# Eight neighbouring weight rows to a partition, 8 KB stage buffers, and another final norm, in a one-core mixture-of-experts block

## The chip, the cores and the metric

The kernel runs on one core of a Trainium2 chip. Its engines are TensorE (PE, with PEld for the weight loads), VectorE (DVE), ScalarE (ACT), GpSimd (POOL) and SyncE (SP, which here only issues DMAs and reads registers). The metric is the device time of one execution in microseconds; lower is better.

## What is computed

A block on x of 2048 tokens by 1024 columns, all float32: a convolution mixer and a gated DeltaNet, an output projection with a residual, a mixture of experts, and a final norm. The change touches the loading of the expert weights, the operand that goes with them, and the final norm:

```python
x = x + jnp.concatenate([y_a, y_b], axis=-1) @ w_out[l]
h = rms_norm(x, ffn_norm_g[l]).reshape(Bsz * S, D)
x = x + hier_moe(h, router_group_w[l], router_expert_w[l], w_gate[l], w_up[l], w_down[l]).reshape(Bsz, S, D)
...
return rms_norm(x, final_norm_g)

def hier_moe(h, ...):
    # a group of 4 is chosen for each token, then the top 2 of its 8 experts: 32 experts in all
    ...
        a = xblk @ w_gate[e]        # [tokens, 1024] @ [1024, 512]
        b = xblk @ w_up[e]
        return (jax.nn.silu(a) * b) @ w_down[e]     # [tokens, 512] @ [512, 1024]
```

## The kernel before

The program has five stretches (times of the profiled execution): projections, DeltaNet and mixers to about 940 us; the output projection, 940 to 1150; routing, to 1187; the expert loop, to 1875; the end of the final norm, to 1951. P is 128 partitions, D 1024, KT = 8 blocks of 128 columns of D, FF 512, NT = 16 token tiles.

**Precision.** Each product is made from float16 pieces. `split` (lines 91 to 93) writes the high piece with ACT (L92: a scaled copy) and then the low piece with DVE (L93: source times scale minus the high piece). Three matmuls take the place of one.

**Output projection.** A loop over 16 token tiles. `tile_a(t)` multiplies by `wo` in two halves of 512 columns (L965), adds the halves to the tile of x on DVE (L970), squares on ACT, writes the sum to DRAM `acc_d`, makes the scale `ss` on POOL (L978), and splits x times `ss` into `hh` (L979), which SP writes to `h2_d`. `tile_b(t - 1)` transposes `hh` and multiplies by the router weights `wr`. SP loads the next tile of x ahead of each. From tile 10 on, `hid` runs `load_picked` beside the tiles, five steps to a tile: it loads the first two experts, picked from the tokens seen by then.

**Weights of an expert.** `load_part` (L757) has three parts: the first and the second half of gate and up (8 steps), and down (4 steps). A step takes one stage buffer of 128 partitions by 4 KB from `stage()`, has SP load it from DRAM, and calls `split` into the float16 tile `wgu` or `wd`. Gate and up are viewed as "(k p) f": partition p gets row k*128 + p, so one step has two DMAs of 128 rows of 2 KB, a gate half and an up half. Down has one DMA of 128 rows of 4 KB. `gw` holds the norm's gain times WS, one column for each k. The pool `mst` has five buffers; after the output projection `mst2` brings five more on the other side of memory, and `stage()` takes them in turn. SP works its queue in order: a DMA that waits for its buffer holds up every DMA written behind it.

**Expert loop.** 32 jobs, one for each expert, by rising number from the two early ones. `weave` interleaves generators by the shares given with each: in job j, `gate_up(J)` (L1045) beside the rest of the weights of job j + 1, then `down(J)` (L1080, L1115) beside the first part of job j + 2. POOL gathers each job's rows of `h2_d` and scatter-adds its result `yo` to `acc_d` (L1058). Each scatter-add waits for the one before.

**Final norm.** `norm_all` (L1339) loads the 16 tiles of `acc_d` with POOL's indirect DMAs (L1347) through index columns `bix`, which leave out the tokens of the last three jobs; it first loads AHEAD = 8 tiles into eight stage buffers. Then come, for each four tiles, the squares, the root and the gains, and the stores: SP for tiles 0 to 11 (L1369), POOL for 12 to 15 (L1371). Behind the store of tile t the load of tile t + 8 is written, in the next stage buffer. That load waits until the store that last read this buffer has landed, and behind `gathers[0]`, the gather of the rows of job 30. The rows of those tokens are done apart: `rows_of` (L1379) gathers them, `norm_rows` and `store_rows` (L1390) finish them; `last_rows` puts the two middle jobs' rows, of 120 and 116 tokens ("ends"), behind the first store of POOL; the last job's 112 rows ("base") come at the very end. Each of these three stores waits for the one before to land, as a token may belong to two of the jobs.

## Time and profile before

| what | us |
|---|---|
| median of three runs | 1953.33 (1951.74 to 1954.88) |
| the profiled execution's own time | 1952.58 |
| its span in the trace | 1950.8 |
| PE busy over the span | 1747.4 (90%) |
| DVE busy | 1402.0 (72%) |
| ACT busy | 1008.3 (52%) |
| POOL busy | 436.7 (22%) |

Execution and span lie 1.8 us apart; a difference read in the span is a difference of the execution. The shares of the whole span say little here, since the stretches have different limits: the table of busy time by stretch has to be read, and inside a stretch the chain of waits, which follows the work that ended last back from its end. PEclk is TensorE's granted clock, 1.00 being 2.4 GHz. The DMA share is the mean busy share of the core's sixteen DMA engines, as their packet records give it; it goes a few hundredths over 1.

### The profile page before, as it was taken

The numbers are of one execution on the slowest core, as the hardware profiler recorded it, in microseconds if no ns is written. First come the engines' busy times: TensorE is split into PE (matmuls) and PEld (weight loads), VectorE is DVE, ScalarE is ACT, GpSimd is POOL, SyncE is SP. The second block draws the span as 40 slices with busy tenths as digits, with TensorE's granted clock in tenths as the row PEclk, the third lists the DMA queues.
The fourth block names the chain that finished last, engine by engine and source line by source line (L and its number), as shares of the span: only waits on it lengthen the run. The fifth ranks groups of instructions, "written<-read, shape, count | busy, mean of one in ns | idle before, by whom it ended". The sixth has DMA issues, their size and how long they took to land.

```text
span 1950.8 us, 41817 instructions
## 1 busy us (share of the span) xinstructions
PE 1747.4 (90%) x16213; PEld 1197.7 (61%) x16213; DVE 1402.0 (72%) x2708; ACT 1008.3 (52%) x1674; POOL 436.7 (22%) x375
## 2 busy tenths in 40 slices
PE   6789999999999999999999869899889999999830
PEld 5455555555555554444454438798888899999730
DVE  8889888888888745322344768787778888888722
ACT  6655434444444324211233636676667877777631
POOL 1321111121121100000000013233222344344343
PEclk9889999999999999999999979999999999999975
DMA  4222002001001105002255967999999999999873
GB/s 143 67 69 52 11 16 52 9 13 45 20 10 37 36 18 165 22 17 60 98 174 182 343 236 254 342 302 312 305 312 346 360 343 343 344 349 309 290 228 140
DMA packets 203597, 330.27 MB, mean 169 GB/s; under 512 B 44590, under 2 KB 98935, under 8 KB 203394
## 3 DMA queue, kind: packets, MB, share of 16 engines
q1 hardware_dynamic: 178738, 271.20, 40.7%
q0 software_dynamic: 20128, 47.30, 9.7%
q10 hardware_dynamic: 4528, 9.06, 1.2%
q8 instruction: 129, 2.11, 0.4%
q14 instruction: 74, 0.61, 0.1%
HBM read 276.05 MB, written 54.82 MB: 170 GB/s over the span
## 4 chain that ended last, share of the span: by engine, by line
PE 35%; DMA 15%; DVE 7%; issue 5%; ACT 3%; SPq 1%; POOL 1%; POOLq 0%; ACTq 0%; DVEq 0%
PE a L1045 12%; PE acc L134 11%; DMA mst<-in_w_up_dram 7%; PE a L965 5%; DMA mst<-in_w_down_dram 4%; DVE wgu L93 2%; ACT wgu L92 1%; DMA mst<-in_w_gate_dram 1%; DMA mst<-acc_d,bix 1%; SPq L766 1%; PE pn L548 1%; PE pl L1102 1%; PE pl L1080 1%; DVE xT L1031 1%; DMA wst<-in_w_out_dram 1%
## 5 line engine op out<-in xcount | busy, mean ns | idle before, releaser
L134 PE MATMUL acc<-hT,whl 128*128 128x512 f16 x2640 | 636.5, 381 | 0.2 <-DVE hT L203 0.2
L134 PEld LDWEIGHTS <-whl 128*128 128x128 f16 x2640 | 253.3, 99 | 249.6 <-issue 13.4
L1045 PE MATMUL a<-xT,wgu 128*128 128x128 f16 (+17 forms) x6144 | 393.8, 227 | 5.0 <-DVE sl L1052 4.1
L1045 PEld LDWEIGHTS <-wgu 128*128 128x128 f16 x6144 | 388.3, 99 | 11.3 <-issue 5.3
L93 DVE SCALAR_TENSOR_TENSOR wgu<-mst,gw,wgu 128x1024 f16<-128x1024 f32 x256 | 317.3, 1276 | 20.7 <-ACT wgu L92 17.9
L92 ACT ACTIVATE wgu<-mst,gw 128x1024 f16<-128x1024 f32 x256 | 280.1, 1139 | 32.6 <-DMA mst<-in_w_up_dram 30.1
L965 PE MATMUL a<-wo,yb 128*128 128x512 f16 x768 | 175.8, 380 | 0.0
L1058 POOL DMA_INDIRECT acc_d<-yo,tabS x50 | 101.5, 2031 | 253.9 <-ACT yo L1106 189.8
L93 DVE SCALAR_TENSOR_TENSOR wd<-mst,wd 128x1024 f16<-128x1024 f32 x128 | 154.1, 1214 | 5.0 <-ACT wd L92 5.0
L92 ACT ACTIVATE wd<-mst 128x1024 f16<-128x1024 f32 x128 | 131.0, 1047 | 22.2 <-DMA mst<-in_w_down_dram 21.4
L1115 PE MATMUL a<-ac,wd 128*128 128x144 f16 (+12 forms) x1824 | 136.2, 230 | 1.3 <-ACT ac L92 1.2
L1115 PEld LDWEIGHTS <-wd 128*128 128x128 f16 x1824 | 124.2, 98 | 4.0 <-issue 2.3
L965 PEld LDWEIGHTS <-yb 128*128 128x128 f16 x768 | 72.0, 98 | 79.2 <-issue 2.4
L294 DVE SCALAR_TENSOR_TENSOR cv<-raw,pcol,cv 128x512 f32<-128x512 f32 x144 | 117.9, 821 | 1.6
L1014 POOL DMA_INDIRECT xr<-h_d,tabG x51 | 59.6, 1168 | 168.9 <-PE t L1030 162.8
L1052 DVE SCALAR_TENSOR_TENSOR sl<-a,sl 128x128 f32<-128x128 f32 (+17 forms) x128 | 38.3, 300 | 78.8 <-ACT sl L1051 78.3
L1051 ACT ACTIVATE sl<-a 128x128 f32<-128x128 f32 (+17 forms) x128 | 35.9, 281 | 113.7 <-PE a L1045 112.9
L382 DVE TENSOR_TENSOR pr<-Ts,fs 32x1 f32<-32x1 f32 (+14 forms) x240 | 77.7, 324 | 3.9 <-DMA fs<-dscr 0.2
L1019 POOL DMA_INDIRECT gs<-gt_d,gix x51 | 74.0, 1451 | 15.6 <-issue 15.3
L1102 PE MATMUL pl<-id,yt 128*128 128x128 f32 (+13 forms) x304 | 53.3, 296 | 25.1 <-ACT yo L1106 20.9
L545 ACT ACTIVATE osq<-acv 128x512 f32<-128x512 f32 x16 | 10.0, 627 | 126.1 <-DVE acv L543 126.1
L1080 PE MATMUL pl<-wd,ac 128*128 128x512 f16 (+4 forms) x312 | 75.0, 387 | 0.2 <-DVE ac L93 0.2
(348 smaller groups left out, 2539.3 us busy)
## 6 DMA issues: line engine op xcount, KB each, us to landing
mst<-in_w_gate_dram SPq DMA_DIRECT2D x256, 256.0 KB
mst<-in_w_up_dram SPq DMA_DIRECT2D x256, 256.0 KB
mst<-in_w_down_dram SPq DMA_DIRECT2D x128, 512.0 KB
wst<-in_w_in_dram SPq DMA_DIRECT2D x28, 512.0 KB
xt<-in_x_dram SPq DMA_DIRECT2D x16, 512.0 KB
ydr<-yh SPq DMA_DIRECT2D x64, 128.0 KB
x<-in_x_dram SPq DMA_DIRECT2D x16, 512.0 KB
yb<-ydr SPq DMA_DIRECT2D x16, 512.0 KB
```

The costliest lines, as they stand in the source:

```text
L92: A.activation(hi, src, AF.Copy, scale=scale)
L93: (eng or V).scalar_tensor_tensor(lo, src, scale, hi, op0=OP.mult, op1=OP.subtract)
L134: T.matmul(acc, w[:, i, k, :], hT[b][:, j, k, :], start=(n == 0), stop=(n == 3 * KT - 1))
L294: V.scalar_tensor_tensor(y, tap(j), pcol[:, q:q + 1], y, op0=OP.mult, op1=OP.add)
L382: V.tensor_tensor(q, Ts[:, 0:i, 0:i].rearrange("p j m -> p m j"), bc(fs[:, None, 0:i, i], [32, i, i]), op=OP.mult)
L965: T.matmul(po, yb[:, i, k, c * P:(c + 1) * P], wo[:, j, k, n * FF:(n + 1) * FF], start=(q == 0), stop=(q == 3 * KT - 1))
L1019: G.indirect_dma_start(out=g[0:cw], out_offset=None, in_=gt_d[0:end * NE, :], in_offset=IO(ap=gx, axis=0))
L1045: T.matmul(pg[:, q, 0:n], wq[:, i, k, q, f * P:(f + 1) * P], xT[:, j, k, 0:n], start=(z == 0), stop=(z == 3 * KT - 1))
L1058: st = G.indirect_dma_start(out=acc_d, out_offset=IO(ap=sx, axis=0), in_=yo[0:cw], in_offset=None, bounds_check=S - 1, oob_is_err=False, c ...
L1080: T.matmul(py[0:n], ac[:, i, k, 0:n], wd[:, j, k, q * FF:(q + 1) * FF], start=(z == 0), stop=(z == 3 * FF // P - 1))
L1102: T.transpose(py[0:cw, c * P:(c + 1) * P], yts[d2][:, u, off:off + cw], id32)
L1115: T.matmul(pg[:, u, 0:n], wd[:, i, k, d * P:(d + 1) * P], ac[:, j, k, 0:n], start=(z == 0), stop=(z == 3 * FF // P - 1))
```

## The change

Three things are done. **Weights:** gate and up are viewed as "(p k) f", so that partition p holds the eight neighbouring rows 8p to 8p + 7. A step of two k then loads 2 x 2 KB that lie side by side in DRAM, one piece of 4 KB for each partition, and a stage buffer is [128, 2, 1024], 8 KB a partition. An expert has 4 DMAs for gate, 4 for up (of 512 KB each, where 8 of 256 KB stood) and 4 for down as before, in pairs to a buffer. `mst` has two such buffers (five of 4 KB before), `mst2` three (five before), and the turn among them is mst, mst2, mst2, mst, mst2. **What goes with them:** k now numbers columns 8p + k of h, so the gains `gw` are loaded in that order by a DMA of their own, the router's weights too, and the split of `hh` reads the tile of x in steps of eight columns (32 bytes) and writes it in rows. **Final norm:** tiles 0 to 7 are loaded in pairs to a stage buffer (`load_early`); tiles 8 to 15 all go into one tile `xw`, which takes a buffer of `wgu` after the last expert's weights (`load_late`), so none waits for a store. The squares, gains and stores of tiles 0 to 3 move ahead of the scatter of job 30, tile 4's store is made to wait for that scatter, and at the end `rest()` does the ends' norms, tiles 8 to 11, the base rows' norm, tiles 12 to 15, and then the stores of the three ends.

```diff
-    mst = moe.enter_context(tc.tile_pool(name="mst", bufs=5, reuse_waits="tile"))
+    mst = moe.enter_context(tc.tile_pool(name="mst", bufs=2, reuse_waits="tile"))
...
-        return pool.tile([P, D], F32, name="mst")
+        return pool.tile([P, 2, D], F32, name="mst")
...
-            vs = [src[0][ds(e, 1)].rearrange("o (k p) f -> p (o k) f", p=P) for src in (w_gate, w_up)]
-            for k in range(i * KT // 2, (i + 1) * KT // 2):
-                st = stage().rearrange("p (q f) -> p q f", q=2)
+            vs = [src[0][ds(e, 1)].rearrange("o (p k) f -> p (o k) f", k=KT) for src in (w_gate, w_up)]
+            for k in range(i * KT // 2, (i + 1) * KT // 2, 2):
+                st = stage().rearrange("p q (k f) -> p q k f", k=2)
                 for q in range(2):
-                    lastw[0] = nc.sync.dma_start(st[:, q], vs[q][:, k, :]).ins
-                split(w[:, 0, k], w[:, 1, k], st, gw[:, k:k + 1])
-                yield 1
+                    lastw[0] = nc.sync.dma_start(st[:, q], vs[q][:, k:k + 2, :]).ins
+                for d in range(2):
+                    split(w[:, 0, k + d], w[:, 1, k + d], st[:, :, d], gw[:, k + d:k + d + 1])
+                    yield 1
...
-            for k in range(FF // P):
+            for k in range(0, FF // P, 2):
                 st = stage()
-                lastw[0] = nc.sync.dma_start(st, v[:, k, :]).ins
-                split(w[:, 0, k], w[:, 1, k], st, WS)
-                yield 1
+                for d in range(2):
+                    lastw[0] = nc.sync.dma_start(st[:, d], v[:, k + d, :]).ins
+                for d in range(2):
+                    split(w[:, 0, k + d], w[:, 1, k + d], st[:, d], WS)
+                    yield 1
...
-        split(hh[:, 0], hh[:, 1], x1, ss)
+        split(*(hh[:, i].rearrange("p (k q) -> p k q", k=KT) for i in range(2)), x1.rearrange("p (q k) -> p k q", k=KT), ss)
...
-    mst2 = moe.enter_context(tc.tile_pool(name="mst2", bufs=5, side="right", reuse_waits="tile"))
-    stages[:] = [mst, mst2]
+    mst2 = moe.enter_context(tc.tile_pool(name="mst2", bufs=3, side="right", reuse_waits="tile"))
+    stages[:] = [mst, mst2, mst2, mst, mst2]
...
+    def load_early():
         for t in range(AHEAD):
+            if t % 2 == 0:
+                pair = stage()
+            xs[t] = pair[:, t % 2]
             load(t)
             yield 1
+
+    def load_late():
+
+        w = mw.tile([P, NT - AHEAD, D], F32, name="xw", tag="wgu")
+        with tc.issue_after(gathers[0]):
+            for t in range(AHEAD, NT):
+                xs[t] = w[:, t - AHEAD]
+                load(t)
...
                 if t < NPL:
-                    nc.sync.dma_start(out2[t * P:(t + 1) * P, :], x)
+                    st = nc.sync.dma_start(out2[t * P:(t + 1) * P, :], xs[t])
+                    if t == GT:
+                        tc.add_manual_dep(st.ins, adds[-1].ins.name, SYNC, reason="the scatter goes first")
...
-                load(t + AHEAD)
...
+    def rest():
+        for x, sx in ends:
+            norm_rows(x)
+        yield from slices(na, 2 * GT)
+        norm_rows(J.base[0][0:J.n], end)
+        yield from slices(na, 2 * GT)
+        for x, sx in ends + [(end, J.chunks[0][2])]:
+            store_rows(x, sx)
```

How the instructions move is shown at three places. **POOL at the last scatter-adds**, as the kernel before has them: L1058 is the scatter-add of job 30, L1379 the gathers of the last jobs' rows, L1347 a load of a token tile, L1334 a root, L1400 the base rows' scatter:

```order
L1058 DMA acc_d<-yo,tabS 2048x1024
L1379 DMA mst<-acc_d,tabG 112x1024
L1379 DMA end<-acc_d,tabG 120x1024
L1379 DMA end<-acc_d,tabG 116x1024
L1347 DMA mst<-acc_d,bix 128x1024 x4
L1334 TENSOR_TENSOR ss_24316<-ss_24316,mhalf 128x4
L1347 DMA mst<-acc_d,bix 128x1024 x2
L1334 TENSOR_TENSOR ss_24429<-ss_24429,mhalf 128x4
L1347 DMA mst<-acc_d,bix 128x1024 x2
L1400 DMA acc_d<-mst,tabS 2048x1024
```

And in the changed kernel (L1063, L1392, L1347, L1339 and L1413 are the same instructions):

```order
L1063 DMA acc_d<-yo,tabS 2048x1024
L1339 TENSOR_TENSOR ss_23741<-ss_23741,mhalf 128x4
L1392 DMA mst<-acc_d,tabG 112x1024
L1392 DMA end<-acc_d,tabG 120x1024
L1392 DMA end<-acc_d,tabG 116x1024
L1347 DMA xw<-acc_d,bix 128x1024 x8
L1413 DMA acc_d<-mst,tabS 2048x1024
```

The eight loads of late tiles now stand in one row behind the gathers, with no root between them.

**POOL at its end**, before: L1371 is a store of a token tile, L1390 a store of an end's rows, L1334 a root:

```order
L1334 TENSOR_TENSOR ss_24472<-ss_24472,mhalf 128x4
L1334 TENSOR_TENSOR ss_24487<-ss_24487,mhalf 120x1
L1371 DMA out_dram<-mst,bix 2048x1024
L1334 TENSOR_TENSOR ss_24493<-ss_24493,mhalf 116x1
L1390 DMA out_dram<-end,tabS 2048x1024
L1371 DMA out_dram<-mst,bix 2048x1024 x2
L1390 DMA out_dram<-end,tabS 2048x1024
L1371 DMA out_dram<-mst,bix 2048x1024
L1334 TENSOR_TENSOR ss_24518<-ss_24518,mhalf 112x1
L1390 DMA out_dram<-mst,tabS 2048x1024
```

And in the changed kernel (L1385 and L1403 are those stores):

```order
L1339 TENSOR_TENSOR ss_23995<-ss_23995,mhalf 120x1
L1339 TENSOR_TENSOR ss_24001<-ss_24001,mhalf 116x1
L1339 TENSOR_TENSOR ss_24007<-ss_24007,mhalf 128x4
L1339 TENSOR_TENSOR ss_24026<-ss_24026,mhalf 112x1
L1339 TENSOR_TENSOR ss_24032<-ss_24032,mhalf 128x4
L1385 DMA out_dram<-xw,bix 2048x1024 x4
L1403 DMA out_dram<-end,tabS 2048x1024 x2
L1403 DMA out_dram<-mst,tabS 2048x1024
```

All roots now stand ahead of all stores, and the three stores of the ends stand last, behind four stores of tiles, where the first of them stood behind one.

**DVE in the output projection beside the load of the picked experts**, before: L970 adds a half of the product to x, L93 makes the low piece of `hh` or of `wgu`, L1000 makes a tile's logits:

```order
L970 SCALAR_TENSOR_TENSOR x_9719<-a,x_9719 128x512
L977 TENSOR_SCALAR ss_10020<-ss_10020 128x1
L93 SCALAR_TENSOR_TENSOR hh<-x_9719,ss_10020,hh 128x1024
L93 SCALAR_TENSOR_TENSOR wgu<-mst,gw,wgu 128x1024
L970 SCALAR_TENSOR_TENSOR x_9888<-a,x_9888 128x512
L93 SCALAR_TENSOR_TENSOR wgu<-mst,gw,wgu 128x1024
L1000 SCALAR_TENSOR_TENSOR L<-pl,lt 128x36
L970 SCALAR_TENSOR_TENSOR x_9888<-a,x_9888 128x512
L93 SCALAR_TENSOR_TENSOR wgu<-mst,gw,wgu 128x1024
L977 TENSOR_SCALAR ss_10162<-ss_10162 128x1
L93 SCALAR_TENSOR_TENSOR wgu<-mst,gw,wgu 128x1024 x2
```

And in the changed kernel (L974 and L1005 are L970 and L1000):

```order
L974 SCALAR_TENSOR_TENSOR x_9719<-a,x_9719 128x512
L981 TENSOR_SCALAR ss_10020<-ss_10020 128x1
L93 SCALAR_TENSOR_TENSOR hh<-x_9719,ss_10020,hh 128x1024
L974 SCALAR_TENSOR_TENSOR x_9888<-a,x_9888 128x512
L93 SCALAR_TENSOR_TENSOR wgu<-mst,gw,wgu 128x1024 x2
L1005 SCALAR_TENSOR_TENSOR L<-pl,lt 128x36
L974 SCALAR_TENSOR_TENSOR x_9888<-a,x_9888 128x512
L981 TENSOR_SCALAR ss_10156<-ss_10156 128x1
L93 SCALAR_TENSOR_TENSOR wgu<-mst,gw,wgu 128x1024 x2
L974 SCALAR_TENSOR_TENSOR x_10028<-a,x_10028 128x512
L93 SCALAR_TENSOR_TENSOR wgu<-mst,gw,wgu 128x1024
```

The pieces of `wgu` now come two in a row from one buffer, where they came singly.

## Rows read from the trace of the kernel before

**Rows 1.** The page's first line.
```profile
span 1950.8 us, 41817 instructions
```

**Rows 2.** Busy time by stretch, all engines; columns in the first line.
```profile
core 0: us, PE busy (x) PEld busy (x) DVE busy (x) ACT busy (x) POOL busy (x), PEclk, DMA share, GB/s
...
1050.00:1170.00 120.00, 93.62 (x652) 48.24 (x651) 81.11 (x216) 61.88 (x78) 11.21 (x15) 0.88 0.77 273
...
1187.00:1500.00 313.00, 289.81 (x3705) 260.96 (x3704) 252.22 (x333) 221.13 (x312) 91.25 (x57) 0.96 0.99 320
...
1500.00:1800.00 300.00, 294.89 (x4535) 281.01 (x4533) 261.23 (x380) 227.98 (x330) 122.41 (x79) 1.00 1.02 344
...
1875.00:1951.00 76.00, 0.00 (x0) 0.00 (x0) 20.40 (x22) 12.31 (x22) 30.81 (x25) 0.51 0.52 170
```

**Rows 3.** Chain that ended last, 1040 to 1200: start, us, what.
```profile
1054.30 1.28 DVE hh L93
...
1069.81 7.44 DMA x<-in_x_dram
...
1090.88 9.18 DMA mst<-in_w_down_dram
...
1120.22 5.48 DMA mst<-in_w_down_dram
...
1147.27 1.30 DVE hh L93
```

**Rows 4.** Busy time in three 2-us stretches, columns as rows 2.
```profile
1077.00:1079.00 2.00, 2.00 (x11) 0.90 (x10) 0.69 (x1) 1.10 (x2) 0.00 (x0) 1.00 1.04 400
...
1326.50:1328.50 2.00, 2.00 (x38) 2.00 (x37) 0.84 (x1) 2.00 (x4) 1.55 (x1) 0.97 1.06 408
...
1086.50:1088.50 2.00, 2.00 (x12) 0.91 (x10) 2.00 (x3) 2.00 (x4) 0.00 (x0) 1.00 1.03 420
```

**Rows 5.** Timeline of SP's queue, 1835 to the end: start, us, instruction.
```profile
1861.76 47.74 SPq L1369 DMA_DIRECT2D out_dram<-mst  x12
```

**Rows 6.** DVE by line and shape, 100 to 700: count | busy, mean ns.
```profile
L382 DVE TENSOR_TENSOR pr<-Ts,fs 32x64 f32<-32x64 f32 x16 | 4.0, 253 | 0.3
...
L382 DVE TENSOR_TENSOR pr<-Ts,fs 32x225 f32<-32x225 f32 x16 | 9.5, 597 | 0.1
```

**Rows 7.** All engines by line and shape, 940 to 1160.
```profile
L93 DVE SCALAR_TENSOR_TENSOR hh<-x,ss,hh 128x1024 f16<-128x1024 f32 x16 | 20.5, 1283 | 20.3 <-ACT hh L92 20.3
...
L92 ACT ACTIVATE hh<-x,ss 128x1024 f16<-128x1024 f32 x16 | 18.3, 1146 | 13.1 <-POOL ss L978 13.1
```

**Rows 8.** By line, 1187 to 1850; behind the bar's second: idle before, releaser.
```profile
L93 DVE SCALAR_TENSOR_TENSOR wgu<-mst,gw,wgu 128x1024 f16<-128x1024 f32 x239 | 295.8, 1276 | 14.5 <-ACT wgu L92 11.9 <-DMA mst<-in_w_gate_dram 2.4
...
L92 ACT ACTIVATE wgu<-mst,gw 128x1024 f16<-128x1024 f32 x238 | 260.2, 1139 | 27.5 <-DMA mst<-in_w_up_dram 25.2 <-DMA mst<-in_w_gate_dram 0.8
```

**Rows 9.** Timeline of POOL from 1838 to the end; brackets: idle before, releaser.
```profile
1879.60 0.98 POOL L1379 DMA_INDIRECT mst<-acc_d,tabG  x1 [15.83 <-DMA acc_d<-yo,tabS]
...
1883.77 1.04 POOL L1347 DMA_INDIRECT mst<-acc_d,bix  x1 [0.30 <-issue]
...
1899.15 1.02 POOL L1347 DMA_INDIRECT mst<-acc_d,bix  x1 [7.10 <-DMA out_dram<-mst]
...
1906.79 2.03 POOL L1347 DMA_INDIRECT mst<-acc_d,bix  x1 [0.30 <-issue]
...
1924.22 2.02 POOL L1390 DMA_INDIRECT out_dram<-end,tabS  x1 [0.23 <-issue]
...
1930.27 1.27 POOL L1390 DMA_INDIRECT out_dram<-end,tabS  x1 [1.41 <-issue]
...
1940.26 1.01 POOL L1390 DMA_INDIRECT out_dram<-mst,tabS  x1 [6.84 <-issue]
```

More of the change, by code (lines that the diff above doesn't have):

```diff
@@ L1246, in overflow @@
         for dst, row in ((cp_, capE), (rk, nov)):
-            pq = stage(mst).rearrange("p (k t e) -> p k t e", k=2, e=NE)
+            pq = stage(mst)[:, 0].rearrange("p (k t e) -> p k t e", k=2, e=NE)
             V.tensor_tensor(pq, OH, bc(row[:, None, None, :], sh), op=OP.mult)
@@ L1276, in overflow @@
         for q in range(2):
-            big = stage(mst).rearrange("p (a b) -> p a b", a=NE)
+            big = stage(mst)[:, 0].rearrange("p (a b) -> p a b", a=NE)
             V.tensor_tensor(big, bc(iot[:, q * NE:(q + 1) * NE, None], sh), bc(oend[:, None, :], sh), op=OP.is_ge)
@@ L1337, in gain, with load, norm_all @@
         V.scalar_tensor_tensor(x if dst is None else dst, x, s, gfin[0:n], op0=OP.mult, op1=OP.mult)
-    def norm_all():
-        xs = {}
-        def load(t):
-            if t < NT:
-                xs[t] = stage()
-                hold = tc.issue_after(gathers[0]) if t >= AHEAD else nullcontext()
-                with hold:
-                    st = G.indirect_dma_start(out=xs[t], out_offset=None, in_=acc_d,
-                                              in_offset=IO(ap=bix[:, t:t + 1], axis=0), bounds_check=S - 1,
-                                              oob_is_err=False)
-                apart(st, adds)
-                for o in sums:
-                    tc.add_manual_dep(st.ins, o.ins.name, SYNC, reason="the sums of the experts before")
-                loads.append(st)
+    xs = {}
+    def load(t):
+        st = G.indirect_dma_start(out=xs[t], out_offset=None, in_=acc_d, in_offset=IO(ap=bix[:, t:t + 1], axis=0),
+                                  bounds_check=S - 1, oob_is_err=False)
+        apart(st, adds)
+        for o in sums:
+            tc.add_manual_dep(st.ins, o.ins.name, SYNC, reason="the sums of the experts before")
+        loads.append(st)
+    def load_early():
         for t in range(AHEAD):
+            if t % 2 == 0:
+                pair = stage()
+            xs[t] = pair[:, t % 2]
             load(t)
             yield 1
+    def load_late():
[4 more added lines that the diff above has]
+                load(t)
+    def norm_all():
         for t0 in range(0, NT, GT):
@@ L1425, in behind @@
             yield z
-    def last_rows(na, ends):
-        for _ in na:
-            if len(stores) == 1 and not outs:
-                for x, sx in ends:
-                    norm_rows(x)
-                for x, sx in ends:
-                    store_rows(x, sx)
-            yield 1
     eids = {}
@@ L1508, in hybrid_block @@
         if left == LAST:
[L1509 to L1511 removed]
+            parts.append((slices(firsts, 4), 4, WE, 1))
         weave(*parts)
[L1513 removed]
+        if left in (LAST, 1):
             marks.append(latest())
[L1515 to L1518 removed]
+    end = stage()[0:J.n, 0]
+    def rest():
[6 more added lines that the diff above has]
+            store_rows(x, sx)
+    drain(behind(rest(), marks[-1]))
     nb_ = nc.values_load(nblk[0:1, 0:1], min_val=0, max_val=NB2)
@@ L1529, in hybrid_block @@
         add(J)
-        x = rows_of(ox[:, 1:2], P, stage())
+        x = rows_of(ox[:, 1:2], P, stage()[:, 0])
         norm_rows(x)
```

51 lines of the change are left out of this document (20 added, 31 removed).

## The prediction

> **What bounds the kernel now.** The page's first line gives the span [rows 1]; the table of busy time by stretch is read next, since the stretches have different limits [rows 2]. In the expert loop two limits stand close together. From 1187 to 1500 the DMA share is 0.99 and PE is busy 289.81 of 313 us at a granted clock of 0.96; from 1500 to 1800 PE is busy 294.89 of 300 while the DMA share is 1.02. So what shortens transfers can pay in the first of these and hardly in the second. In the end of the output projection (1050 to 1170) neither is full: PE 93.62 of 120, DMA 0.77. There the chain of waits has to be read [rows 3]: it runs over the landing of a tile of x (7.44 us), of down pieces (9.18 and 5.48), and over the split of `hh` on DVE. From 1875 on PE has nothing to do, and the end is a chain of POOL's transfers, read from POOL's timeline [rows 9].
>
> **The end of the final norm.** POOL stands 15.83 us until the scatter of job 30 has landed, then issues the gathers and the late loads [rows 9]. The first late load starts at 1883.77 and each takes 1.04 and 0.30 of issue. But the sixth waits 7.10 us for a store, at 1899.15, and the last starts at 1906.79, since the later loads need buffers that stores must free. With `xw` the eight run in a row: the last starts at 1883.77 + 7 x 1.34 = 1893.2, 13.6 us sooner. Against that, four tile stores instead of one now stand ahead of the first end's store: 3 x (1.02 + 0.30) = 4.0 later. What is behind stays: 6.05 from the first end's store to the second (1924.22 to 1930.27), 9.99 to the third (1940.26), 10.5 to the end of the span. Third, the stores of tiles 0 to 3, which began at 1861.76 [rows 5] and moved while POOL stood for the scatter, now come before it, and tiles 4 and on wait for it: 2.1 MB, 5.1 us at the 408 GB/s of [rows 4], are out of its way; I take 2 of the 5. Sum -13.6 + 4.0 - 2 = -11.6, taken as **-12**. Ends: if the second interval shrinks to the first's 6.05, as no tile store stands between, and the scatter gains 4, it is -9.6 - 3.9 - 4 = -17.5, so -18; if the ends' stores find their queue full it is -1 (a rival, below).
>
> **Pieces of 4 KB.** In two saturated stretches of 2 us, rows of 2 KB went at 408 GB/s, and in one where rows of 4 KB filled the queue it was 420, the share at its top in both (1.06 and 1.03) [rows 4]. An expert's gate and up are 4.19 MB: 10.28 us at 408, 9.99 at 420, so 0.29 an expert. 239 splits of `wgu` at 8 an expert are 30 experts [rows 8], 8.8 us if every one were bound by the transfer. The second stretch is bound by PE, so about half is to be had: **-5** (-9 to 0; 0 since the stretch's mean of 320 [rows 2] lies well under 408, so that something other than the packet rate may set it). The four DMA issues an expert that SP saves are worth nothing, as SP waits for buffers anyway.
>
> **Coarser stage buffers.** A buffer of 4 KB is held for a split, 1.139 on ACT and then 1.276 on DVE [rows 8], 2.4 us. One of 8 KB is held for two, which overlap: 1.139 + 2 x 1.276 = 3.7. So 1.3 us more pass until a buffer takes its next load. Five buffers of 1 MB stand for ten of 512 KB, 5.2 MB either way, 12.8 us of queue at 408; the 1.3 us should mostly be covered by the other four. What is late if not is ACT, which already stood 25.2 us for up pieces in this stretch [rows 8]. I take **+3**, an eighth of that; 0 if all is covered, +8 if the wait grows by a third.
>
> **The split of `hh` in steps of 32 bytes.** DVE's product in L382 reads both its sources in steps of 64 bytes: 253 ns for 64 elements, 597 for 225 [rows 6], so 344 / 161 = 2.14 ns an element. The split of `hh` takes 1283 ns for 1024 elements in a row [rows 7]; at 2.14 it is 2.19 us, 0.9 more. All sixteen grow, but up to 1050 PE hides them. Five stand on the chain from 1040 to 1150, the first at 1054.30, the last at 1147.27 [rows 3]: **+4**. The trace has no such read on ACT; its piece is 1146 ns [rows 7]. If it grows by 0.9 too the sum is +9; if four of five find cover in the landings between, +1. The Trainium skill, "Vector Engine (DVE) Microarchitecture Reference", section 5.2, tells of this cost: single words that hop on one source take 1.73 ns a column, where pairs or rows take 1.05. [Rows 6] have two such sources, at 2.14. By the page's figure the split would be 0.6 longer, my estimate, and this term +3.
>
> **Two experts through two buffers.** Until 1170 only `mst` is there: two of 8 KB, where five of 4 KB were. The queue is deep there: a piece of 512 KB needs 1.28 us at 408, but 9.18 passed from its issue to its landing [rows 3]. With 2.1 MB outstanding instead of 2.6 the queue is 1.3 us shorter, and the tile of x behind it lands sooner; but SP stands longer for a buffer with that x written behind it, and both pieces of a buffer land before either is split. The three landings shown are 22.1 us. I take **+3**; if they grow by half it is +11, taken as +12 with the second wait for `hh`, and if they shrink by a quarter, -6. The DMA for `gw` and the new view of the router's weights are small and lie before 940, behind projections: 0. The extra wait of tile 4's store for the scatter holds up only SP's stores behind it, which the late loads no longer need: 0, with the tail's range for what they cost on the queue.
>
> Sum: -12 - 5 + 3 + 4 + 3 = -7. From the profiled execution, 1952.58, that gives 1945.6; the median of the three runs lies 0.75 above it, so **1946** as a median.
>
> **Rivals.**
> *The preload stalls the projection tiles* (slower). Place: 1050 to 1170. Price: the landings grow by half to double, say +14 instead of +3, and `hh` costs +9: 1952.58 - 12 - 5 + 3 + 9 + 14 = 1961.6, about 1962. For it: PE is idle there for 26 us already, and every tile's end waits for ACT and DVE, which hold the pieces in order. Against it: fewer bytes are outstanding and no byte is added. It decides once these terms pass 14 us together.
> *The ends' stores eat the gain.* They now stand behind four tile stores, 2.1 MB or 5.1 us of queue, and if both intervals become 9.99: 1893.2 + 17.4 (last load to first end's store, as before) + 4.0 + 5.1 + 2 x 9.99 + 10.5 = 1950.2, the tail gains 1 and the sum is +4: about 1957. Against it: tile stores went between the ends before too.
> *The pieces move more than 0.29 an expert* (faster). If 4 KB pieces took the transfers off the path from 1187 to 1500, PE would no longer idle there (23.2 us), the clock's 0.04 (12.5) and the 5.1 of the next stretch would come back: 41 us instead of 5, about 1910. [Rows 4] speak against it: the saturated rates differ by 3%. The Trainium skill, "Perfetto Trace Analysis", section "DMA Optimizations", says that going from 2 KB to 4 KB or 8 KB can dramatically improve throughput; by that rule this rival would be the likeliest, and by [rows 4] it is not.
> *Pieces 16 KB apart are slower* (slower). Neighbouring partitions now read 16 KB apart instead of 2. No row has that pitch. If such pieces went at the first stretch's mean of 320 [rows 2] and not 408, an expert's gate and up would be 13.1 us, +2.8, for 14 experts there (313 of 663 us for 30) +39, and no -5: about 1990. The Trainium skill, "DMA: Bandwidth & Descriptors", section "Latency and other measured facts", has rates that fall at row pitches of large powers of two, its mildest 207 of 214 GB/s at 512 KiB; 16 KB it does not list.
> *It does not do what it says*, that is, the rate of 4 KB pieces is no better: 1951, inside the forecast's range.
>
> **How the numbers follow.** Chances: the forecast 0.47 (1936 to 1952), the stalled preload 0.20, the ends' stores 0.20, the fast pieces 0.08, the 16 KB pitch 0.05. All low ends together would give -32, all high ones +27, which is not likely at once: I cut to 1928 and 1966, which leaves out the two last rivals and the far end of the first, 0.19. A measurement of this kernel can tell about 0.2%, 3.9 us. Faster by more: 0.40 of the forecast, 0.08, 0.04 of the ends' stores, 0.01 of the preload: 0.53. Within: 0.07 + 0.10 + 0.03 = 0.20. Slower: 0.05 + 0.16 + 0.06 = 0.27.
>
> **What would show it.** In the profile after: the eight late loads in a row and the last at about 1893 less what earlier stretches gained; the first end's store some ten us sooner by the same measure; the span from there on unchanged at 26 us. Rates in saturated stretches of gate and up at 410 to 420 and not 408; the split of `hh` at 2.2 us on DVE, and its ACT piece longer or not; the landings on the chain from 1040 to 1150 near 22 us in sum; ACT's idle time before up pieces at 25 to 33 us. I would be wrong above all if the expert loop as a whole moved by more than 10 us, as my terms for it come from small differences, or if the projection's end, where I have only bounds, grew by more than 15.

## The result and the profile after

The changed kernel is **slower**, by 0.56%: 1963.48 us (median of 5 runs, 1961.66 to 1968.19) against 1953.33, a ratio of 1.0056 (95% interval 1.0034 to 1.0078). The forecast was 1946, faster; the time lies inside its range and on the other side of no change. The profiled execution has a span of 1959.9, 9.1 more than [rows 1]. From here on times are given as ratios to the kernel before on the same chip, as its median differs between chips (1949.3 to 1955.8); 0.1% is 2 us. All runs have five rounds, or four where it is said.

The page's first line, and the busy time by stretch, with the columns of [rows 2]:

```profile
span 1959.9 us, 40611 instructions
```

```profile
core 0: us, PE busy (x) PEld busy (x) DVE busy (x) ACT busy (x) POOL busy (x), PEclk, DMA share, GB/s
...
1050.00:1170.00 120.00, 91.88 (x627) 46.60 (x627) 82.14 (x191) 68.51 (x76) 6.64 (x11) 0.89 0.77 260
...
1187.00:1500.00 313.00, 286.56 (x3672) 255.40 (x3669) 247.16 (x330) 215.86 (x309) 85.00 (x56) 0.97 0.94 313
...
1500.00:1800.00 300.00, 294.69 (x4527) 280.99 (x4525) 260.46 (x381) 225.58 (x329) 123.16 (x79) 1.00 1.01 343
...
1875.00:1960.00 85.00, 14.13 (x170) 11.67 (x167) 22.63 (x32) 16.16 (x35) 29.10 (x26) 0.61 0.53 173
```

The first stretch has the same DMA share and less PE. In the second the DMA share fell from 0.99 to 0.94 while the rate fell too, from 320 to 313 GB/s [rows 2]: a byte takes 3% less of the queue (0.94 / 313 against 0.99 / 320), which is what larger pieces should do, but the queue stands empty more often. (A byte's share of the queue is the DMA share divided by the rate.) In the last stretch PE still works 14 us where it had nothing left to do.

Where the 9.1 us arise is read from POOL's timeline: the scatter-adds of job 0, of job 29 and of job 30, first of the kernel before (its L1058), then of the changed one (L1063). The numbers are start, duration, instruction. A bracket is idle time before the instruction and what ended it.

```profile
1190.78 2.13 POOL L1058 DMA_INDIRECT acc_d<-yo,tabS  x1 [5.47 <-ACT yo L1089]
...
1852.39 1.69 POOL L1058 DMA_INDIRECT acc_d<-yo,tabS  x1 [0.30 <-ACT ac L92]
...
1860.65 3.12 POOL L1058 DMA_INDIRECT acc_d<-yo,tabS  x1 [0.24 <-issue]
```

```profile
1198.44 2.13 POOL L1063 DMA_INDIRECT acc_d<-yo,tabS  x1 [5.48 <-ACT yo L1094]
...
1862.71 1.64 POOL L1063 DMA_INDIRECT acc_d<-yo,tabS  x1 [0.30 <-issue]
...
1877.87 2.17 POOL L1063 DMA_INDIRECT acc_d<-yo,tabS  x1 [7.21 <-ACT sl L1056]
```

| until | before | after | difference |
|---|---|---|---|
| router product of the last token tile | 1151.4 | 1156.5 | +5.1 |
| scatter of job 0 | 1190.78 | 1198.44 | +7.7 |
| scatter of job 29 | 1852.39 | 1862.71 | +10.3 |
| scatter of job 30 | 1860.65 | 1877.87 | +17.2 |
| end of the span | 1950.8 | 1959.9 | +9.1 |

So 7.7 come before the first job has ended, 2.6 in the whole expert loop, 6.9 between two scatters at its end, and the final norm gives 8.1 back. The first and the third have a row each. Over the output projection, the split of `hh`, as [rows 7]:

```profile
L92 ACT ACTIVATE hh<-x,ss 128x1024 f16<-128x1024 f32 x16 | 34.3, 2146 | 9.7 <-POOL ss L982 9.6
...
L93 DVE SCALAR_TENSOR_TENSOR hh<-x,ss,hh 128x1024 f16<-128x1024 f32 x16 | 33.2, 2073 | 26.7 <-ACT hh L92 26.6
```

ACT's piece grew by 1.00 us and DVE's by 0.79. On the chain from 1040 to 1160 five DVE pieces stand as before, and three ACT pieces where there were two (1.16 us each, at 1128.69 and 1146.08). Start, us, what:

```profile
1052.14 2.07 DVE hh L93
...
1063.03 9.39 DMA mst<-in_w_up_dram
...
1086.78 2.00 DVE hh L93
...
1094.08 9.04 DMA mst<-in_w_down_dram
...
1108.20 2.15 ACT hh L92
...
1110.37 2.09 DVE hh L93
...
1116.40 6.32 DMA mst<-in_w_up_dram
...
1125.08 1.61 ACT hh L92
...
1130.72 2.06 DVE hh L93
...
1149.42 2.13 ACT hh L92
...
1151.58 2.07 DVE hh L93
```

At the loop's end it is ACT's timeline that tells (L1335 is a tile's square, L92 a piece of `ac`, L1094 one of `yo`):

```profile
1863.90 1.06 ACT L1335 ACTIVATE jk<-mst 128x1024 f16<-128x1024 f32 x1 [3.54 <-DMA mst<-acc_d,bix]
...
1864.95 0.47 ACT L92 ACTIVATE ac<-sl 128x116 f16<-128x116 f32 x2
...
1871.58 1.06 ACT L1335 ACTIVATE jk<-mst 128x1024 f16<-128x1024 f32 x1 [3.00 <-DMA mst<-acc_d,bix]
...
1874.21 0.67 ACT L1094 ACTIVATE yo<-pl,gs 116x512 f32<-116x512 f32 x1
...
1903.54 1.06 ACT L1335 ACTIVATE jk<-end 120x1024 f16<-120x1024 f32 x1 [15.44 <-DMA end<-acc_d,tabG]
...
1909.87 1.06 ACT L1335 ACTIVATE jk<-end 116x1024 f16<-116x1024 f32 x1 [5.19 <-DMA end<-acc_d,tabG]
```

The squares of tiles 0 to 7 now stand in ACT's order ahead of job 30's pieces. At 1863.90 and 1871.58 a square waits for its tile to land, 3.54 and 3.00 us, and `ac` and `yo` wait behind it. The scatter needs `yo`. The last two rows are the squares of the ends' rows, which wait for their gathers. Then POOL's end, answering [rows 9] (L1392 a gather of the last jobs' rows, L1347 a late load, L1339 the root of tiles 12 to 15, L1403 the stores of the ends):

```profile
1891.82 1.02 POOL L1392 DMA_INDIRECT mst<-acc_d,tabG  x1 [10.70 <-DMA acc_d<-yo,tabS]
...
1910.11 0.99 POOL L1347 DMA_INDIRECT xw<-acc_d,bix  x1 [5.24 <-DMA end<-acc_d,tabG]
...
1925.19 1.02 POOL L1339 TENSOR_TENSOR ss<-ss,mhalf 128x4 f32<-128x4 f32 x1 [7.00 <-DVE ss L1338]
...
1934.85 1.03 POOL L1403 DMA_INDIRECT out_dram<-end,tabS  x1 [0.30 <-issue]
...
1939.65 1.27 POOL L1403 DMA_INDIRECT out_dram<-end,tabS  x1 [3.77 <-DMA out_dram<-end,tabS]
...
1949.42 0.96 POOL L1403 DMA_INDIRECT out_dram<-mst,tabS  x1 [8.50 <-DMA out_dram<-end,tabS]
```

From the first gather to the last late load it was 27.2 us [rows 9] and is 18.3, but from that gather to the first end's store it was 44.6 and is 43.0, and from there to the end of the span 26.6 and 25.0. Nearly all that the earlier loads gained is lost again before the first store. Two waits in these rows take it. The last late load waits 5.24 us for a gather of the ends' rows, and the root of tiles 12 to 15 waits 7.00 us for DVE. DVE's timeline shows what it does meanwhile (L1342 a gain, L1338 the sum of a tile's squares):

```profile
1916.51 2.48 DVE L1342 SCALAR_TENSOR_TENSOR end<-end,ss,gfin 120x1024 f32<-120x1024 f32 x2
1918.91 4.87 DVE L1342 SCALAR_TENSOR_TENSOR xw<-xw,ss,gfin 128x1024 f32<-128x1024 f32 x4
1923.69 1.28 DVE L1342 SCALAR_TENSOR_TENSOR mst<-mst,ss,gfin 112x1024 f32<-112x1024 f32 x1
1924.88 0.16 DVE L1338 TENSOR_SCALAR ss<-ss 128x4 f32<-128x4 f32 x1
```

In the order of `rest()` the gains of the ends, of tiles 8 to 11 and of the base rows stand ahead of the sum that the last root needs, though ACT was done with the last squares at 1920.6.

### The profile page after: what moved, and what is told of

It reads as the page before. It is cut to its first block, busy times and chain, and to the rows that moved or that the text cites. A ratio compares the mean times of both kernels' runs of the same rounds, so it can differ in the third digit from the quotient of the medians.

```text
span 1959.9 us, 40611 instructions
## 1 busy us (share of the span) xinstructions
PE 1753.1 (89%) x16213; PEld 1200.2 (61%) x16213; DVE 1414.2 (72%) x2708; ACT 1020.3 (52%) x1674; POOL 423.7 (22%) x375
## 4 chain that ended last, share of the span: by engine, by line
PE 34%; DMA 12%; DVE 10%; issue 6%; ACT 5%; POOL 1%; SPq 0%; POOLq 0%; ACTq 0%; DVEq 0%
PE a L1050 12%; PE acc L134 10%; DMA mst<-in_w_up_dram 7%; PE a L969 5%; DMA mst<-in_w_down_dram 3%; DVE wgu L93 3%; ACT wgu L92 2%; PE pl L1107 1%; PE pn L548 1%; DVE xT L1036 1%; DMA wst<-in_w_out_dram 1%; DVE yt L1126 1%; PE t L1035 1%; ACT yo L1111 1%; DVE wd L93 1%
## 5 line engine op out<-in xcount | busy, mean ns | idle before, releaser
L93 DVE SCALAR_TENSOR_TENSOR wgu<-mst,gw,wgu 128x1024 f16<-128x1024 f32 x256 | 317.1, 1276 | 24.0 <-ACT wgu L92 23.6
L92 ACT ACTIVATE wgu<-mst,gw 128x1024 f16<-128x1024 f32 x256 | 278.6, 1138 | 41.5 <-DMA mst<-in_w_up_dram 39.7
L93 DVE SCALAR_TENSOR_TENSOR wd<-mst,wd 128x1024 f16<-128x1024 f32 x128 | 154.2, 1215 | 4.9 <-ACT wd L92 4.7
L1063 POOL DMA_INDIRECT acc_d<-yo,tabS x50 | 95.8, 1917 | 267.4 <-ACT yo L1111 193.3
L92 ACT ACTIVATE wd<-mst 128x1024 f16<-128x1024 f32 x128 | 130.7, 1047 | 19.5 <-DMA mst<-in_w_down_dram 19.4
```

Source lines behind the costliest of these rows:

```text
L92: A.activation(hi, src, AF.Copy, scale=scale)
L93: (eng or V).scalar_tensor_tensor(lo, src, scale, hi, op0=OP.mult, op1=OP.subtract)
L1063: st = G.indirect_dma_start(out=acc_d, out_offset=IO(ap=sx, axis=0), in_=yo[0:cw], in_offset=None, bounds_check=S - 1, oob_is_err=False, c ...
```

## Experiments

### The final norm alone, and its order

First the changed norm in the kernel before, with nothing else of the change.

> The kernel before with the changed final norm alone; weights, layout and stage buffers as before. Theory: the tail from the scatter of job 30 to the end shrinks by about 8 us, as in the changed kernel (90.2 to 82.0), but the squares of tiles 0 to 7 now stand in ACT's order ahead of job 30's ac pieces and yo pieces and wait for their tiles, so that scatter starts about 7 us later: in sum -1, about 1952 (1949 to 1955). Rival 1 (the record's sum): only the tail counts, -12, about 1941. Rival 2: the late scatter of job 30 in the changed kernel came from the coarser stage buffers, which deliver the early tiles later; then here the scatter is not late and the time is about -8, 1945.

Measured: 0.9991 (0.9977 to 1.0005), so about -2 us where the prediction had -12. Its POOL timeline has the late scatter without any coarse buffer, which drops the second rival:

```profile
1868.94 2.17 POOL L1058 DMA_INDIRECT acc_d<-yo,tabS  x1 [7.92 <-ACT sl L1051]
...
1882.87 1.02 POOL L1385 DMA_INDIRECT mst<-acc_d,tabG  x1 [10.67 <-DMA acc_d<-yo,tabS]
```

The scatter of job 30 starts 8.3 us later than before (0.7 of it from earlier stretches), and the time from there to the end is 81.5 where it was 90.1. Then the early squares back behind job 30's pieces:

```diff
-            parts += [(firsts, AHEAD - 4, 0, 0.5), (behind(slices(na, 2 * GT), marks[0]), 2 * GT, 0.5, 1)]
+            parts.append((firsts, AHEAD - 4, 0, 1))
...
-            parts.append((behind(slices(na, 2 * GT), marks[1] + [adds[-1].ins]), 2 * GT, 0, 1))
+            parts += [(behind(slices(na, 2 * GT), marks[1]), 2 * GT, 0, 0.6),
+                      (behind(slices(na, 2 * GT), marks[2] + [adds[-1].ins]), 2 * GT, 0.6, 1)]
```

> As the run with the changed final norm alone, but the squares, gains and stores of tiles 0 to 7 are written where the kernel before had them, behind job 30's ac pieces. Theory: the 7 us of the late scatter are gone and the 8 us of the tail stay: about 1945 (1942 to 1948). Rival (squares on ACT are not the cause): no better than the run with the changed norm alone, about 1952.

Measured: 0.9988 (0.9973 to 1.0004). The theory fell in its second half. The scatter is on time: it starts 8.2 us after that of job 29, as before, where the run above has 15.9. (The whole profile runs early, by 4.1 us at the scatter of job 0 and 6.8 at that of job 29.) But POOL stands 16.63 for it to land, not 10.67, and the time from its start to the end is 89.3, so the 8 us of the tail are gone:

```profile
1853.86 3.12 POOL L1058 DMA_INDIRECT acc_d<-yo,tabS  x1 [0.24 <-issue]
...
1873.61 0.99 POOL L1385 DMA_INDIRECT mst<-acc_d,tabG  x1 [16.63 <-DMA acc_d<-yo,tabS]
```

So the order on ACT did delay the scatter, but undoing that won nothing, as the scatter then took longer. By the packet records SP's stores moved 2.1 MB while it ran, and 0.26 MB in the run above; that the stores slow it is the likely reading, not tested apart. A second guess was the order of the ends' squares, which stand ahead of eight tiles' squares on ACT and wait 15.44 and 5.19 for their gathers (the last two rows of ACT above, from the changed kernel):

```diff
     def rest():
-        for x, sx in ends:
-            norm_rows(x)
         yield from slices(na, 2 * GT)
         norm_rows(J.base[0][0:J.n], end)
         yield from slices(na, 2 * GT)
+        for x, sx in ends:
+            norm_rows(x)
```

> The changed norm on the old weights (0.9991), with one thing moved: the squares, roots and gains of the ends' rows come behind those of all late tiles and not ahead of them. In the changed kernel ACT stood 15.4 and 5.2 us for the gathers of the ends' rows with eight squares of tiles queued behind, and the last root came 15 us after the last late load. Theory: that order took what the earlier loads had gained; with it undone the first end's store comes 4 to 7 us sooner and the ratio is 0.996. Rival: the tail's transfers (the gather of 116 rows, which POOL's last late load waits for too) set it whatever the order: 0.999.

Measured: 0.9987 (0.9976 to 0.9997), the rival's number. POOL's last late load itself waits 5.82 for the gather of the ends' rows, and the first end's store comes at 1925.43, as in the first of these runs (1925.54). The last root did start 1.2 us sooner (1914.67 against 1915.88), but the ends' two roots stand behind it on POOL, ahead of the tile stores. The rival's reason, the transfers, is put to the test next.

### The 116 rows of job 30

Three transfers of the tail have 116 rows: the scatter, the gather and the store of job 30. Busy time in 10 us in which that scatter runs, before and after (columns as [rows 2]; the last two are the DMA share and GB/s):

```profile
1870.00:1880.00 10.00, 4.13 (x20) 2.21 (x17) 0.25 (x1) 0.00 (x0) 0.40 (x1) 0.81 0.24 60
```

```profile
1880.00:1890.00 10.00, 7.32 (x64) 6.03 (x64) 6.53 (x12) 1.64 (x7) 1.12 (x2) 0.83 0.25 41
```

SP's stores wait for the scatter in the changed kernel, so hardly anything else moves, and the sixteen engines are busy a quarter of the time, as four of them would be; the profile does not say which. One number was changed, in the changed norm on old weights and in the kernel before:

```diff
-            132, 132, 128, 128, 124, 124, 124, 120, 120, 120, 116, 112]
+            132, 132, 128, 128, 124, 124, 124, 120, 120, 120, 120, 112]
```

> The changed norm on the old weights, and job 30 has 120 rows instead of 116. The tail is a chain of transfers of job 30's and its neighbours' rows: its scatter (POOL stands 10.7 us for it), the gather of its rows (15.2) and its store (8.4). Theory: an indirect transfer of 116 rows is spread over few DMA engines and one of 120 rows over many, so each of the three shrinks, and the end comes 8 to 15 us earlier: about 0.994. Rival: the three are bound by latency or by the other transfers, then 0.999.

Measured (four rounds): **0.9891** (0.9869 to 0.9913). This is more than expected. POOL stands 4.94 for the scatter instead of 10.67, and 3.31 for the second end's store (job 30's rows) instead of 8.41. Of the rows below, the three in the middle are the last late load, the root of tiles 12 to 15 and the first end's store:

```profile
1867.21 0.98 POOL L1385 DMA_INDIRECT mst<-acc_d,tabG  x1 [4.94 <-DMA acc_d<-yo,tabS]
...
1880.20 0.99 POOL L1342 DMA_INDIRECT xw<-acc_d,bix  x1 [0.30 <-issue]
...
1898.79 1.01 POOL L1334 TENSOR_TENSOR ss<-ss,mhalf 128x4 f32<-128x4 f32 x1 [11.78 <-DVE ss L1333]
...
1908.43 1.02 POOL L1396 DMA_INDIRECT out_dram<-end,tabS  x1 [0.30 <-issue]
...
1917.43 0.95 POOL L1396 DMA_INDIRECT out_dram<-mst,tabS  x1 [3.31 <-DMA out_dram<-end,tabS]
```

The trace's packet records show the same from the side of the transfers. The scatter of 116 rows moves 101 packets of 4 KB in 10.6 us (1871.69 to 1882.25), 3.6 of them in flight on average; with 120 rows it is 101 packets in 3.8 us (1862.84 to 1866.62), 11.9 in flight. A packet takes 328 ns (median) in both. The store of 116 rows has 3.1 in flight and takes 7.1 us, that of 120 rows 11.4 and 2.1; the base rows' store, of 112 rows, has 10.9 in the changed kernel. So it is not the time of a packet but how many run at once, which drops the rival of latency. Which other numbers of rows are slow was not tried.

The gather shows the limit of this. With 120 rows the last late load waits for nothing (0.30) and starts 13.0 us after the first gather, where it was 18.1. Yet the first end's store comes 41.2 us after that gather, where it was 42.7, since the root of tiles 12 to 15 now waits 11.78 for DVE, which makes eleven gains in a row ahead of that sum (1885.32 to 1898.57). So between the gathers and that store the work on DVE binds the changed norm, and not the transfers; no run changed DVE's order as a whole.

> The kernel before with 120 rows in job 30 instead of 116 and nothing else. Theory: the same three transfers stand on the chain of the old final norm too, but its late loads still wait for stores, so about two thirds of the 21 us come: ratio 0.992 to 0.994. Rival: the old norm hides none or gains all, 0.989; or its stores bind it, 0.997.

Measured: **0.9847** (0.9832 to 0.9863), 1925.44 us, more than expected. The scatter is followed by the first gather 10.58 us after its start, where it was 18.95:

```profile
1853.66 2.63 POOL L1058 DMA_INDIRECT acc_d<-yo,tabS  x1 [0.24 <-issue]
...
1864.24 0.97 POOL L1379 DMA_INDIRECT mst<-acc_d,tabG  x1 [7.95 <-DMA acc_d<-yo,tabS]
```

Where the two runs gained, from POOL's timelines (us; one profile each):

| stretch | old norm, 116 rows | old norm, 120 | changed norm, 116 | changed norm, 120 |
|---|---|---|---|---|
| to the scatter of job 29 | 1852.39 | 1844.25 | 1853.07 | 1843.29 |
| to the scatter of job 30 | 8.26 | 9.41 | 15.87 | 17.31 |
| to the first gather | 18.95 | 10.58 | 13.93 | 6.61 |
| to the first end's store | 44.62 | 38.81 | 42.67 | 41.22 |
| to the end of the span | 26.58 | 20.55 | 24.86 | 19.07 |

The scatter gave 8.4 and 7.3 us, the stores at the end 6.0 and 5.8. But 8.1 of 27.2 and 9.8 of 22.9 us had come before the scatter of job 29, ahead of the three transfers. Part of that is the spread of executions: the scatter of job 0, up to which these kernels do the same, comes at 1186.5 to 1191.8. But from there to the scatter of job 29 the four profiles with 116 rows (the kernel before and the three of its changed norm) have 659.0 to 661.8 us, and the four with 120 (these two and the two below) 655.3 to 656.7. So some 5 us more come from inside the expert loop. The gather of job 30's rows of `h2_d` lies there and has 116 rows too; that it brings them was not tested.

Two further versions of the changed norm with 120 rows: the ends' stores ahead of the tiles' stores (the edit below), and with it the early squares late, by the same edit as above.

```diff
-    NPL = NT - GT
+    NPL = NT - 2 * GT
...
         for x, sx in ends:
             norm_rows(x)
+        store_rows(*ends[0])
         yield from slices(na, 2 * GT)
+        store_rows(*ends[1])
         norm_rows(J.base[0][0:J.n], end)
-        yield from slices(na, 2 * GT)
-        for x, sx in ends + [(end, J.chunks[0][2])]:
-            store_rows(x, sx)
+        yield from slices(na, GT + 1)
+        store_rows(end, J.chunks[0][2])
+        yield from slices(na, GT - 1)
```

> As the run with 120 rows in job 30, and tiles 8 to 11 are stored by POOL like 12 to 15, so that the three stores of the ends need not wait for them: the first stands ahead of all tile stores, the second behind four, the third behind five. In that run the three serial stores began at 1908.4 and ended the span at 1927.5, 19 us that nothing else needed. Theory: they now run beside the tile stores and the end comes 8 to 14 us earlier, ratio 0.983 to 0.985. Rival: the tail is bound by the tiles' squares and gains or by bytes, then no more than 3 us: 0.988.

> The run with 120 rows and earlier ends' stores (0.9855), with the squares of tiles 0 to 7 behind job 30's ac pieces as in the kernel before, so that its scatter is not 9 us late. Theory: most of those 9 us come back now that no transfer of 116 rows stands behind them: 0.981 to 0.983. Rival: as in the run with 116 rows the scatter then shares the queue with the stores of tiles 0 to 3 and lands no sooner: 0.985, no better than the kernel before with 120 rows.

Measured: 0.9855 (0.9839 to 0.9871) and 0.9879 (0.9860 to 0.9899), medians 1925.91 and 1925.25. The first lies between its theory and its rival; the second is no better than the first, as its rival had it. Neither is better than the one number in the kernel before (0.9847), and the first cannot be told from it.

### The layout in parts

The layout of the weights with all that goes with it, in 2 KB pieces through the old buffers; then the split of `hh` alone; then the addresses alone. The last two give products of unmatched columns; the work is the same.

> The kernel before with the eight-neighbour layout alone (gains, router weights and the split of hh with it), still in pieces of 2 KB through ten buffers of 4 KB; final norm as before. Theory: only the split of hh costs, about +4 at the end of the output projection, and the expert loop runs as before: 1957 (1955 to 1959). Rival 1: 2 KB pieces that lie 16 KB apart load more slowly, the loop grows by 5 us or more: 1962 and above. Rival 2: the late end of the output projection is the preload through two buffers, then 1954.

> The kernel before with the split of hh in steps of 32 bytes (and gains and router weights in that order), while the experts' weights keep rows k*128 + p; the experts' products are thus of unmatched columns, the work is the same. The layout as a whole cost 0.75% (about 14 us by medians, 10 between the profiles). Theory: the split of hh costs its longer pieces on ACT and DVE at the end of the output projection, +4 to +6, and nothing in the expert loop: ratio 1.0025. Rival: all of it, 1.007, then the addresses of the weights cost nothing.

> The kernel before with the experts' gate and up rows viewed as eight neighbours to a partition and nothing else (2 KB pieces 16 KB apart, ten buffers of 4 KB; hh in rows, so that the products are of unmatched columns, the work is the same). Theory: a 2 KB packet of these loads takes on average 3 to 4 ns more, as in the run with the whole layout (96.4 against 93.0 from 1190 to 1500), the loop's transfer-bound part grows by about 5 us and the preload by 1 to 3: ratio 1.0035. Rival: the addresses cost nothing, 1.000.

Measured: 1.0075 (1.0056 to 1.0095), and with four rounds 1.0057 (1.0038 to 1.0076) and 1.0028 (1.0010 to 1.0045). The parts add up to the whole within their intervals. Where the split of `hh` costs is seen at the router product of the last token tile: 1155.1 in the run of the split alone, 1151.4 before. The addresses cost 0.28% by the times, but the packet records do not show where. A 2 KB packet took 96.4 ns on average from 1190 to 1500 in the whole layout, against 93.0 before; in the run of the addresses alone it was 94.8, and in three runs with the old addresses 94.1 to 94.6, so this measure moves as much without the addresses.

The coarse buffers with the old layout (beside the changed norm), and the changed kernel with its pieces cut to 2 KB, which doubles the DMAs too (the edit of the second):

```diff
-                    lastw[0] = nc.sync.dma_start(st[:, q], vs[q][:, k:k + 2, :]).ins
+                    for d in range(2):
+                        lastw[0] = nc.sync.dma_start(st[:, q, d], vs[q][:, k + d, :]).ins
```

> The changed final norm and the changed stage buffers (two and three of 8 KB, two steps to a buffer), but the old layout, hh in rows and 2 KB pieces. Beside the run with the changed norm alone this shows what the coarse buffers cost. Theory: some 3 us in the preload and 2 in the loop: ratio to before 1.0015 to 1.003. Rival 1 (the preload stalls on two buffers): +10 or more at the end of the output projection, 1.005. Rival 2: nothing, 0.999.

> The changed kernel with each gate or up piece of 4 KB loaded by two DMAs of 2 KB rows; addresses, buffers and norm as changed. From the runs so far: split of hh +0.57%, the eight-neighbour addresses in 2 KB rows +0.28%, coarse buffers +0.22% (0.13 + 0.09), norm -0.09%, sum +0.98%, where the changed kernel has +0.56%. Theory: the 4 KB pieces are worth those 0.4%, and this run is at 1.009 to 1.010. Rival: the four are not additive and the pieces are worth nothing, 1.006.

Measured: 1.0013 (0.9998 to 1.0029, four rounds), against 0.9991 for the norm alone, so +0.22% for the buffers; and 1.0076 (1.0061 to 1.0091) against the 1.0056 of the changed kernel, so -0.2% for the 4 KB pieces. Both differences are about as large as the intervals. In the profile of the 2 KB pieces the router product of the last token tile comes at 1166.0, 9.5 us behind the changed kernel (1156.5), and from the scatter of job 0 to that of job 29 it is 666.1 us against 664.3. So what the larger pieces were worth lay in the load of the first experts, hardly in the expert loop. The parts, +0.57 +0.28 +0.22 -0.20 -0.09, sum to +0.78% where +0.56% was measured; each is uncertain by some 0.2, so this is no contradiction.

### Other places for the reordering of columns

`hh` in rows again, and the transposes on PE read every eighth column; or the split reads in rows and writes in steps of 256 bytes.

```diff
...
-                    T.transpose(px[:, k, 0:cw], xr[0:cw, i, k, :], id16[0:cw, 0:cw])
+                    T.transpose(px[:, k, 0:cw], xr[0:cw, i].rearrange("p k c -> p (k c)").rearrange("p (q k) -> p k q", k=KT)[:, k],
+                                id16[0:cw, 0:cw])
```

> The changed kernel, but hh is split and stored in rows as before, and the transposes read every eighth column instead (on PE, float16, steps of 16 bytes). Theory: ACT's and DVE's pieces of hh go from 2.15 and 2.07 us back to 1.15 and 1.28, and of the 5.1 us that the output projection ends late about 4 go: 1963.5 - 4 = 1959.5 (1957 to 1962). Rival 1: the 5.1 us are the preload's two buffers, no gain: 1963. Rival 2: PE reads such columns slowly, and every transpose of the expert loop costs more: 1968 or more.

> The changed kernel, but the split of hh walks its source in rows and writes in steps of 256 bytes (float16) instead of reading in steps of 32 bytes. Theory: hopping costs on the write side too, ACT's and DVE's pieces stay near 2 us and the ratio stays at 1.005 to 1.006. Rival: writes of two bytes hop freely, the pieces go back to 1.15 and 1.28 us and the 0.57% go: 1.000.

Measured: 1.0082 (1.0064 to 1.0100) and 1.0495 (1.0477 to 1.0513). In the first the router product of the last tile came back from 1156.5 to 1153.2, but the expert loop lost more: 678.5 us from the scatter of job 0 to that of job 29, where the changed kernel has 664.3. A weight load of `xr` takes 146 ns (first row), 98 before (second), and PE is busy 295.92 of the 300 us from 1500 to 1800. The 340 loads of the row alone are 340 x 48 ns = 16 us more, an estimate that fits the loss.

```profile
L1035 PEld LDWEIGHTS <-xr 128*128 128x128 f16 x340 | 22.8, 146 | 0.0
```

```profile
L1030 PEld LDWEIGHTS <-xr 128*128 128x128 f16 x352 | 20.7, 98 | 0.0
```

In the second the split of `hh` takes 4.8 us on both engines:

```profile
L92 ACT ACTIVATE hh<-x,ss 128x1024 f16<-128x1024 f32 x16 | 77.5, 4843 | 9.7 <-POOL ss L982 9.6
...
L93 DVE SCALAR_TENSOR_TENSOR hh<-x,ss,hh 128x1024 f16<-128x1024 f32 x16 | 76.4, 4775 | 66.6 <-ACT hh L92 61.8 <-ACT rm L901 4.7
```

## Why the prediction was wrong, step by step

**The final norm, -12: wrong, -2 measured.** This is the step that failed. Three readings in it were wrong, and a fourth was too small. (1) The early norms were priced only as stores out of the scatter's way. That their squares would stand ahead of job 30's pieces in ACT's order, waiting for tiles that had not landed, was put at nothing; it cost 7.6 us at the scatter in the run of the norm alone (6.9 in the changed kernel). The run with those squares moved back had the scatter on time. (2) The late loads were to run in a row, 13.6 us sooner; the last one waited 5.24 for the gather of the ends' rows, and 8.9 came. (3) "What is behind stays" took the first end's store to follow the last late load by the old 17.4 us, and 4.0 for three more tile stores. It was 24.7 (1910.11 to 1934.85), 3.3 more than that, since DVE's gains stand ahead of the sum for the last root, which waited 7.00. With 120 rows (2) went and (3) took its place, 28.2 us with a wait of 11.78. (4) The scatter with the stores out of its way was given 2 us and took 5.0 less. From the first end's store on, where nothing was forecast, 1.5 came. In sum -13.6 + 4.0 - 2 was to be -12, and 6.9 - 8.9 + 7.3 - 5.0 - 1.5 = -1.2 came in the profile.

What the forecast left out besides is the price of the 116 rows. [Rows 9] has it, 15.83 us of POOL's idle time ended by that scatter, and I took it as given. The runs with 120 rows were 1.5% faster in the old norm, more than the whole change moved in either direction; about half of that lies in the scatter and the stores of the tail.

**The split of `hh`, +4: right mechanism, under-sized, +11 (0.57%).** In the profile of that part alone the scatter of job 30 starts 4.6 us late and the span is 5.9 longer, so the size is uncertain between 5 and 15. DVE's 0.79 lies near the 0.9 from [rows 6]. What I left out of the value and kept only as an end was ACT. Two of its pieces stood on the chain before, which [rows 3] does not show; its piece grew more, by 1.00, and three stand there now. The Trainium skill's 1.73 ns a column ("Vector Engine (DVE) Microarchitecture Reference", section 5.2), which is for hops of 4 KiB, gave +0.6 for DVE by my estimate; the trace has (2073 - 1283) / 1024 = 0.77 ns more an element, between the page and [rows 6].

**Pieces of 4 KB, -5: -4 (0.2%), as far as it can be told, but not in its place.** The 3% of [rows 4] is there: among steps of 2 us from 1190 to 1490 the fullest with rows of 4 KB alone went at 416 GB/s (1210 to 1212), and in the kernel before the fullest with hardly any but rows of 2 KB at 408, as in [rows 4]. But the rate over the stretch did not rise (313 GB/s), and the expert loop where the 5 us were to be had did not shrink: 664.3 us from the scatter of job 0 to that of job 29, where it was 661.6. By the run with 2 KB pieces the gain lay in the load of the first experts. That the sum came out at 4 is luck.

**Coarser buffers and the preload through two of them, +3 and +3: +4 (0.22%).** The size held. ACT's wait for up pieces grew from 25.2 [rows 8] to 33.2 us, the third that I had made an end:

```profile
L92 ACT ACTIVATE wgu<-mst,gw 128x1024 f16<-128x1024 f32 x238 | 258.8, 1137 | 35.0 <-DMA mst<-in_w_up_dram 33.2 <-issue 1.3
```

That is not the buffers alone, though: it is 28.6 in the run of the coarse buffers and 31.9 in that of the whole layout through the old ones. So where the 0.22% arises is open. With the split of `hh` in the same stretch these terms make the rival of the stalled projection tiles, at about 1962, the nearest of all forecasts. That is luck too: the landings did not grow by half, the three longest on the chain are 9.39, 9.04 and 6.32, 24.8 us against 22.1. What was late at the projection's end, 5.1 us, came mostly through the split on ACT and DVE (3.7 in its run alone; 1.6 in that of the coarse buffers).

**Pieces 16 KB apart: taken as 0 with a chance of 0.05 at +39, measured +5 (0.28%).** The rival was drawn too large to be likely; a small cost of the same cause should have been a term of its own.

With the norm at -2 in place of -12 the sum is +3 instead of -7, and with `hh` at +9 (my own upper end) too it is +8; 9.1 was measured between the profiles and 0.56%, 11 us, by the times. So the final norm is the step that turned the sign. (The high ends of the prediction add up to +28, not +27; nothing hangs on it.)

## What to carry to other kernels

Before a transfer is given an earlier start, look at what the chain's last transfers are made of: here 116 rows kept the DMA engines a quarter busy, and one number brought 1.5% where reordering brought nothing. An operation that is moved ahead takes its wait with it into an engine's order, and what is written behind it waits too. When transfers come earlier, ask which engine has to work on what they bring, and in what order; here DVE's gains took back what the loads had won. A new data layout has to be paid for somewhere by reordering; price that on every engine that touches it, before the gain in the transfer.

## What the runs showed of the hardware

While an indirect transfer of 116 rows ran, the sixteen DMA engines were 25% busy, at 41 GB/s; with 120 rows the wait for the same scatter fell from 10.67 to 4.94 us. On average 3.6 packets of 4 KB were in flight with 116 rows and 11.9 with 120, at 328 ns a packet in both. For 128 x 1024 elements, reading float32 in steps of 32 bytes took ACT 2146 ns (1146 in rows) and DVE 2073 (1283); writing float16 in steps of 256 bytes took 4843 and 4775. Weight loads of PE from columns 16 bytes apart took 146 ns instead of 98.
